# Reordered casts of K and a larger product fill ahead of two groups of transposes in a streaming encoder step

## The chip, the cores and the metric

The kernel runs on one core of a Trainium2 chip. The metric is the device time of one execution in microseconds (us). A time is the median over several executions; one further execution is recorded by the hardware profiler, and all rows below come from that one.

## What is computed

One step of a one-layer encoder over 1024 frames of a new stream and 64 frames of a running one (together T = 1088 columns), in float32. With `x` the normalised input:

```python
q, k, v, gb, gc, h = project_in(xp, w_in[l])            # six pieces of 512 columns each
attn = prompt_attention(q, k, v, rel_bias, lam)         # 4 heads
def probs(qi, ki):
    s = einsum('bqhd,bkhd->bhqk', qi, ki) * scale + bias
    return softmax(where(visible, s, -inf))
p = probs(q[..., :64], k[..., :64]) - lam * probs(q[..., 64:], k[..., 64:])
attn = einsum('bhqk,bkhd->bqhd', p, v)                  # then a norm per head
conv = gb * causal_conv(gc * h, conv_w)
x = LN(alpha * x + concat(attn, conv) @ w_out)
x = LN(alpha * x + relu(x @ w_ff1)**2 @ w_ff2)
```

Each head has two score maps, from two halves of 64 query and key channels. The 64 sample frames also see 256 cached keys and values. K and V are outputs as well.

## The kernel before

**Numbers in two parts.** A float32 matmul operand is held as a high part (a cast to fp32r) and a low part (value minus high part), and a product is made of three matmuls: high by high, high by low, low by high. ACT makes the high parts with a cast, DVE (for weights POOL) the low parts with a subtraction that reads the high part.

**Stages.** First the input norm and the projections of V and of head 0; then the attention, head by head; then the output projection, the first MLP matmul in Strassen form, and the second. The change touches the attention, and in it the K casts that begin during the first stage.

**Projections as fill.** A projection unit (`uq`, `uk`, `uv` with the number of the head, and `uc`, `uh`, `ub` for the convolution) covers three column chunks of 384, 384 and 320. `chunk_gen` (L270) makes one chunk: 24 matmuls, one `yield` after each, into one PSUM bank of tag `pj`, which has two banks. After the last one it calls the evacuation: for K that is `ek` (L331), which copies the chunk to `kf` in SBUF on ACT and calls `dup_split`. 24 products later (`K_LAG`) `store` (L341) transposes the chunk out of `kf` through the one PSUM bank of tag `tr`, for the output.

**`dup_split` (L322)** writes, for both halves m of 64 channels, the high part twice (own partitions and the other half's partitions) into `kh`, and the low part twice into `kl`, so that a score is two matmuls of a query that holds high and low parts stacked. All eight instructions read the PSUM bank of the chunk. For the cached keys `cache` (L372) does the same into `kc` from an SBUF tile `pcs`.

**Attention of a head (`attention_gen`, L703).** The 1024 queries go in four pairs j of 128-row blocks. For each block `score` (L611) makes two score tiles (tag `sc`, two buffers), and `softmax_diff` (L558) turns them into the difference of two softmax maps, tile `a<head><block>e`: DVE adds the bias and takes the row minimum (`a..m`), ACT takes the exponential, DVE scales and combines; L578 is the combination, in halves of 512 columns. `pv_gen` (L631) then goes through groups g of 256 keys: `tr(g)` transposes the group out of the `a..e` tiles of the pair's two blocks (L642) into the PSUM bank of tag `tr`, ACT and DVE split it into `th` (high and low), and `mm(g)` multiplies it with V. The transposes of group g + 1 stand before the products of group g.

**The order of PE is written by hand.** `attention_gen` and `pv_gen` yield a key ahead of each piece of PE work: `("t", j, g)` ahead of the transposes of group g of pair j, `("o", j, g)` ahead of its products, `("s", i, m)` ahead of a score. The main loop asks the table `FILL` for the key and first takes that many products from the fill:

```python
for w in attention_gen(h, qk, v):
    if w is None: ...                       # after the last scores: uk of the next head joins the fill
    for _ in range(fill_of(h, w)):
        next(fill, None)
run(fill)                                   # what is left
```

The fill of a head holds convolution units, then `uv` and `uq` of the next head, and from the last score on `uk` of the next head (72 products), which may not come earlier, since `kh` and `kl` have one buffer. The orders of ACT, DVE, POOL and SP are not written by hand: a scheduler sets them from the program.

Of the kernel before, what the change touches and what calls it, by code (L numbers as in the profile page):

```python
# [13 lines left out]
ALU = mybir.AluOpType  # L14
# [90 lines left out]
def f32(ap):  # L105
    return ap.bitcast(F32)


def build(tc, a, o):
    nc = tc.nc  # L110
    ctx = ExitStack()
    with ctx:
# [191 lines left out]
        with tc.tile_pool(name="pa", bufs=1, side="right", reuse_waits="tile") as pa:  # L304

            def qk_gens(h):
# [11 lines left out]
                kh = pa.tile([128, 2, T], F32R, name=f"kh{h}", tag="kh")  # L318
                kl = pa.tile([128, 2, T], F32R, name=f"kl{h}", tag="kl")
                kf = pa.tile([128, T], F32, name=f"kf{h}", tag="kf")  # L320

                def dup_split(p, h4, l4):  # L322
                    for m in range(2):
                        me = slice(64 * m, 64 * m + 64)
                        ot = slice(64 - 64 * m, 128 - 64 * m)
                        nc.scalar.copy(out=h4[m][me], in_=p[me])
                        nc.scalar.copy(out=h4[m][ot], in_=p[me])
                        nc.vector.tensor_tensor(out=l4[m][me], in0=p[me], in1=f32(h4[m][me]), op=ALU.subtract)
                        nc.vector.tensor_tensor(out=l4[m][ot], in0=p[me], in1=f32(h4[m][me]), op=ALU.subtract)

                def ek(c, t0, n, p):  # L331
                    s = slice(t0, t0 + n)
                    nc.scalar.copy(out=kf[:, s], in_=p[:, :n])
                    dup_split(p[:, :n], [kh[:, m, s] for m in range(2)], [kl[:, m, s] for m in range(2)])
                    later.append([K_LAG, lambda: store("k", c, t0, n)])

                def ev(c, t0, n, p):
# [3 lines left out]
                def store(kind, c, t0, n):  # L341
                    pk = ps.tile([128, 4, 128], F32, name=f"{kind}t{h}{c}", tag="tr")
                    full, rest = divmod(n, 128)
                    if kind == "k":
                        ks = pa.tile([128, 3, 128], F32, name=f"ks{h}{c}", tag="ks", bufs=2)
                        dst, tail = ks[:, :full, :], ks[:64, full, :] if rest else None
                    else:
                        dst, tail = vst[:, t0 // 128:t0 // 128 + full, :], vs[:64, 2, :]
                    for q in range(full + (rest > 0)):
                        w = min(128, n - q * 128)  # L350
                        nc.tensor.transpose(pk[:w, q, :], kf[:, t0 + q * 128:t0 + q * 128 + w], ident)
                    nc.scalar.copy(out=dst, in_=pk[:, :full, :])
                    nc.sync.dma_start(out=o[f"new_{kind}_prompt"][0, 0, t0:t0 + 128 * full, h, :]
                                      .rearrange("(b p) v -> p b v", p=128), in_=dst)
                    if rest:
                        nc.scalar.copy(out=tail, in_=pk[:64, full, :])
                        nc.sync.dma_start(out=o[f"new_{kind}_sample"][0, 0, :, h, :], in_=tail)
# [10 lines left out]
                kc = pa.tile([128, 2, 2, PAST], F32R, name=f"kc{h}", tag="kc")  # L368
# [3 lines left out]
                def cache():  # L372
                    pc = ps.tile([128, 2, 128], F32, name=f"pc{h}", tag="tr")
                    for q in range(2):
                        nc.tensor.transpose(pc[:, q, :], ck[:, q, :], ident)
                    pcs = pa.tile([128, PAST], F32, name=f"pcs{h}", tag="ks", bufs=2)
                    nc.scalar.copy(out=pcs, in_=pc.rearrange("p b t -> p (b t)"))
                    dup_split(pcs, [kc[:, m, 0, :] for m in range(2)], [kc[:, m, 1, :] for m in range(2)])

                held = {}  # L380

# [6 lines left out]
                def lazy(which, c, evac):  # L388
                    yield from chunk_gen(weights(which), x0, c, f"{which}{h}", evac)

                gens = {which: [lazy(which, c, evac) for c in cs]
                        for which, evac, cs in (("uq", eq, range(3)), ("uk", ek, range(3)), ("uv", ev, range(VX // 3, 3)))}
                return (qs, kh, kl, kc, vst, vs), gens, cache, weights, load_v

            with tc.tile_pool(name="p0", bufs=1, reuse_waits="tile") as p0:
# [1100 lines left out]
```

## Time and profile before

| what | value |
|---|---|
| median of 3 timed runs | 1269.4 us (1269.03 to 1272.67) |
| the profiled execution, its own time | 1265.8 us |
| its span, first to last instruction | 1264.0 us |
| mean granted clock of TensorE over the span | 0.984 of full speed |
| DVE busy | 934.0 us (74%) |
| ACT busy | 535.0 us (42%) |
| the chain that ended last, by engine | PE 68%, DVE 11%, ACT 3%, DMA 2% |

How to read it: a busy share is an average over stages with different limits, so the sections of the trace around one place tell more than the table. The chain is the work that ended last, followed back from the last instruction. The granted clock tells which of TensorE's two levels (1.2 or 2.4 GHz) a stretch ran at: 0.50 is the lower and 1.00 the upper. Matmuls overlap in the pipeline, so the distance from one start to the next, not the listed duration, is what a product takes of PE's time.

### The profile page before, as it was taken

What the parts mean: (1) busy time and instruction counts of PE and PEld (TensorE: products, weight loads), DVE (VectorE), ACT (ScalarE), POOL (GpSimd) and SP (SyncE); (2) the same over time, 40 slices, a digit from 0 to 9 for tenths busy, and PEclk for the clock granted to TensorE, in tenths of its full rate; (3) what the DMA queues carried; (4) which work ended last, traced back from release to release, by engine and by line L of the source; (5) the groups of instructions that cost most, each with busy time, mean ns of one, the idle gap of its engine ahead of it and who ended that gap; (6) DMA issues with size and microseconds to landing.
All of it is one profiled execution on the core that took longest, in us unless ns stands there. A gap on an engine that the chain in (4) does not pass through costs nothing.

```text
span 1264.0 us, 18518 instructions
## 1 busy us (share of the span) xinstructions
PE 1201.9 (95%) x7162; PEld 1088.7 (86%) x7162; DVE 934.0 (74%) x1639; ACT 535.0 (42%) x1037; POOL 93.5 (7%) x53
## 2 busy tenths in 40 slices
PE   7999999989999999988999999999999999999994
PEld 5888899989889878868999999999878888888873
DVE  7855955966866977798867676766667688777897
ACT  4454564664664632144333333332444423323523
POOL 3130211111110000000000000000000000000004
PEclk9999999989999999988999999999999999999997
DMA  7861221212222353305453535352895546334203
GB/s 240 277 188 46 85 69 44 70 55 74 65 60 85 98 166 123 107 34 166 143 183 105 184 105 184 105 168 72 280 336 207 199 134 213 126 120 150 67 17 124
DMA packets 118802, 166.61 MB, mean 132 GB/s; under 512 B 9453, under 2 KB 86297, under 8 KB 115130
## 3 DMA queue, kind: packets, MB, share of 16 engines
q1 hardware_dynamic: 118714, 165.43, 39.8%
q8 instruction: 56, 0.92, 0.3%
q14 instruction: 32, 0.26, 0.1%
HBM read 112.20 MB, written 55.57 MB: 133 GB/s over the span
## 4 chain that ended last, share of the span: by engine, by line
PE 68%; DVE 11%; ACT 3%; DMA 2%; issue 1%; SPq 0%; DVEq 0%; ACTq 0%
PE P L1321 21%; PE py L835 7%; PE fa L1005 5%; PE fa L1007 5%; PE fa L1009 5%; PE fc L1009 2%; PE fc L1005 2%; PE fc L1007 2%; PE fb L1007 1%; PE fb L1005 1%; PE fb L1009 1%; DVE hl L1174 1%; DVE wl L1174 1%; PE smP L1360 1%; PE smP L1359 1%
## 5 line engine op out<-in xcount | busy, mean ns | idle before, releaser
L1321 PE MATMUL P<-wh,hh 128*128 128x512 f32 x448 | 174.6, 390 | 3.8 <-DVE t L1247 3.0
L1321 PE MATMUL P<-wl,hh 128*128 128x512 f32 x448 | 174.5, 389 | 0.7 <-DVE wl L1174 0.7
L1321 PE MATMUL P<-wh,hl 128*128 128x512 f32 x448 | 174.4, 389 | 0.0
L1321 PEld LDWEIGHTS P<-wh,hh 128*128 128x128 f32 x448 | 84.1, 188 | 21.9 <-issue 3.2
L1321 PEld LDWEIGHTS P<-wl,hh 128*128 128x128 f32 x448 | 84.1, 188 | 18.6 <-DVE wl L1174 1.1
L1321 PEld LDWEIGHTS P<-wh,hl 128*128 128x128 f32 x448 | 84.1, 188 | 17.5
L1328 DVE TENSOR_TENSOR x<-x,P 128x512 f32<-128x512 f32 x96 | 64.3, 681 | 37.1 <-PE P L1321 36.8
L1172 ACT CAST hh<-hr 128x1024 fp32r<-128x1024 f32 (+1 forms) x28 | 37.2, 1356 | 109.6 <-PE P L1321 105.4
L1005 PE MATMUL fc<-x,wP 128*128 128x272 f32 x256 | 75.0, 293 | 3.1 <-ACT wP L204 2.6
L1009 PE MATMUL fc<-x,wP 128*128 128x272 f32 x256 | 74.9, 293 | 1.6 <-DVE wP L205 1.5
L1007 PE MATMUL fc<-x,wP 128*128 128x272 f32 x256 | 74.7, 292 | 0.0
L1411 POOL TENSOR_TENSOR x<-x 128x1024 f32<-128x1024 f32 x6 | 14.3, 2379 | 792.0 <-DVE x L1409 786.8
L1174 DVE TENSOR_TENSOR hl<-hr,hh 128x1024 fp32r<-128x1024 f32 (+1 forms) x28 | 44.7, 1602 | 27.6 <-ACT hh L1172 27.6
L1005 PEld LDWEIGHTS fc<-x,wP 128*128 128x128 f32 x256 | 49.2, 192 | 4.0 <-ACT wP L204 3.3
L1009 PEld LDWEIGHTS fc<-x,wP 128*128 128x128 f32 x256 | 49.3, 192 | 2.2 <-DVE wP L205 2.2
L1007 PEld LDWEIGHTS fc<-x,wP 128*128 128x128 f32 x256 | 49.2, 192 | 0.0
L1172 ACT CAST hh<-x 128x1024 fp32r<-128x1024 f32 (+1 forms) x13 | 17.6, 1383 | 50.3 <-PE P L1321 40.1
L1005 PE MATMUL fa<-xt3h,wP 128*128 128x272 f32 x128 | 37.1, 290 | 0.9 <-ACT t L1048 0.9
L1005 PE MATMUL fa<-xt4h,wP 128*128 128x272 f32 x128 | 36.9, 288 | 1.1 <-DVE t L1056 1.1
L1007 PE MATMUL fa<-xt2l,wP 128*128 128x272 f32 x128 | 37.4, 293 | 0.0
L1005 PE MATMUL fa<-xt2h,wP 128*128 128x272 f32 x128 | 37.4, 292 | 0.0
L1009 PE MATMUL fa<-xt2h,wP 128*128 128x272 f32 x128 | 37.3, 292 | 0.0
(1483 smaller groups left out, 3780.2 us busy)
## 6 DMA issues: line engine op xcount, KB each, us to landing
hr<-hv SPq DMA_DIRECT2D x19, 1024.0 KB, 5.0
hv<-hS SPq DMA_DIRECT2D x63, 256.0 KB, 4.2
w2B<-in_w_ff SPq DMA_DIRECT2D x11, 1024.0 KB, 6.5
hv<-hb SPq DMA_DIRECT2D x42, 256.0 KB, 2.7
x<-hv SPq DMA_DIRECT2D x9, 1024.0 KB, 5.0
f1r<-in_w_ff SPq DMA_DIRECT2D x17, 512.0 KB, 4.1
f1k<-in_w_ff SPq DMA_DIRECT2D x14, 512.0 KB, 5.1
x<-in_w_ff SPq DMA_DIRECT2D x6, 1024.0 KB, 6.0
```

The lines of the kernel that those rows point to most:

```text
L835: nc.tensor.matmul(py[:, s], lhsT=(ml if m == 2 else mh)[:, e, :], rhs=wo[e][m == 1][:, s], start=(n == 0), stop=(n == len(ops) - 1))
L1005: nc.tensor.matmul(out, lhsT=w[:, 0, k, :], rhs=xh[:, k, cs], start=first and k == 0, stop=False, skip_group_check=not first)
L1007: nc.tensor.matmul(out, lhsT=w[:, 0, k, :], rhs=xl[:, k, cs], start=False, stop=False, skip_group_check=not first)
L1009: nc.tensor.matmul(out, lhsT=w[:, 1, k, :], rhs=xh[:, k, cs], start=False, stop=last and k == 3, skip_group_check=not first)
L1172: nc.scalar.copy(out=hi[q], in_=src[:, w * q:w * q + w])
L1174: nc.vector.tensor_tensor(out=lo[q], in0=src[:, w * q:w * q + w], in1=f32(hi[q]), op=ALU.subtract)
L1321: nc.tensor.matmul(out, lhsT=x[f][:, c], rhs=w[f], start=new and f == 0 and n == 0, stop=f == GP - 1 and n == 2, skip_group_check=not new)
L1328: nc.vector.tensor_tensor(out=dst, in0=dst, in1=out, op=ALU.add)
L1359: nc.tensor.matmul(out, lhsT=st, rhs=wh[f], start=f == 0, stop=False)
L1360: nc.tensor.matmul(out, lhsT=st, rhs=wl[f], start=False, stop=f == GP - 1)
L1411: nc.gpsimd.tensor_tensor(out=y[:rows], in0=y[:rows], in1=b, op=ALU.add)
```

## The change

Three places. The table entries of `("t", 3, 0)`, the transposes of the first group of the last block pair, go from 8 to 22 products in head 0 and from 2 to 20 in head 1. `dup_split` gets a second source `src`, which is `kf` for a K chunk and the same `pcs` for the cached keys. It now first casts each half to its own partitions, then makes all four low parts, and last casts each half to the other half's partitions, reading `src`. The number of instructions is the same.

```diff
-    (0, 'r', 2, 0): 0, (0, 't', 3, 0): 8, (0, 'o', 3, 0): 0, (0, 't', 3, 1): 12, (0, 'o', 3, 1): 0,
+    (0, 'r', 2, 0): 0, (0, 't', 3, 0): 22, (0, 'o', 3, 0): 0, (0, 't', 3, 1): 12, (0, 'o', 3, 1): 0,
...
-    (1, 't', 3, 0): 2, (1, 'o', 3, 0): 0, (1, 't', 3, 1): 11, (1, 'o', 3, 1): 0, (1, 't', 3, 2): 5,
+    (1, 't', 3, 0): 20, (1, 'o', 3, 0): 0, (1, 't', 3, 1): 11, (1, 'o', 3, 1): 0, (1, 't', 3, 2): 5,
...
-                def dup_split(p, h4, l4):
+                def dup_split(p, src, h4, l4):
+
+                    own = [slice(64 * m, 64 * m + 64) for m in range(2)]
                     for m in range(2):
-                        me = slice(64 * m, 64 * m + 64)
-                        ot = slice(64 - 64 * m, 128 - 64 * m)
-                        nc.scalar.copy(out=h4[m][me], in_=p[me])
-                        nc.scalar.copy(out=h4[m][ot], in_=p[me])
-                        nc.vector.tensor_tensor(out=l4[m][me], in0=p[me], in1=f32(h4[m][me]), op=ALU.subtract)
-                        nc.vector.tensor_tensor(out=l4[m][ot], in0=p[me], in1=f32(h4[m][me]), op=ALU.subtract)
+                        nc.scalar.copy(out=h4[m][own[m]], in_=p[own[m]])
+                    for m in range(2):
+                        for part in own[m], own[1 - m]:
+                            nc.vector.tensor_tensor(out=l4[m][part], in0=p[own[m]], in1=f32(h4[m][own[m]]), op=ALU.subtract)
+                    for m in range(2):
+                        nc.scalar.copy(out=h4[m][own[1 - m]], in_=src[own[m]])
...
-                    dup_split(p[:, :n], [kh[:, m, s] for m in range(2)], [kl[:, m, s] for m in range(2)])
+                    dup_split(p[:, :n], kf[:, s], [kh[:, m, s] for m in range(2)], [kl[:, m, s] for m in range(2)])
...
-                    dup_split(pcs, [kc[:, m, 0, :] for m in range(2)], [kc[:, m, 1, :] for m in range(2)])
+                    dup_split(pcs, pcs, [kc[:, m, 0, :] for m in range(2)], [kc[:, m, 1, :] for m in range(2)])
```

The changed file has two lines more in `dup_split`, so every later line has a number that is higher by two (L642 becomes L644).

PE, head 0, ahead of the transposes `t` of block pair 3 (`a06e` and `a07e` are the softmax maps of blocks 6 and 7, `uq1p` the products of head 1's query projection, `vt` the store of V). Before:

```order
L279 MATMUL uq1p_1686<-x_121,uq1h 128x384
L282 MATMUL uq1p_1686<-x_121,uq1l 128x384
L642 MATMUL t_1732<-ident,a06e_1571 128x128
L642 MATMUL t_1732<-ident,a07e_1705 128x128
L642 MATMUL t_1732<-ident,a06e_1571 128x128
L642 MATMUL t_1732<-ident,a07e_1705 128x128
L276 MATMUL uq1p_1686<-x_121,uq1h 128x384
L279 MATMUL uq1p_1686<-x_121,uq1h 128x384
```

and in the changed kernel:

```order
L279 MATMUL uq1p_1686<-x_121,uq1h 128x384
L353 MATMUL vt_1743<-ident,kf_979 128x128 x2
L353 MATMUL vt_1743<-ident,kf_979 64x128
L282 MATMUL uq1p_1686<-x_121,uq1l 128x384
L276 MATMUL uq1p_1756<-x_121,uq1h 128x384
L279 MATMUL uq1p_1756<-x_121,uq1h 128x384
L644 MATMUL t_1759<-ident,a06e_1571 128x128
L644 MATMUL t_1759<-ident,a07e_1705 128x128
L644 MATMUL t_1759<-ident,a06e_1571 128x128
```

The store of V, the end of the first `uq1p` chunk and the first products of the next now stand ahead of the transposes, where before they stood behind them.

DVE, head 1, the low parts `th` of the transposed groups of pair 3 (`kl` is the low part of K for head 2). Before:

```order
L578 SCALAR_TENSOR_TENSOR a17e_2825<-a17e_2833,a17r_2838,a17e_2825 128x512
L205 TENSOR_TENSOR th_2858<-t_2853,th_2858 128x512
L205 TENSOR_TENSOR th_2877<-t_2872,th_2877 128x512
L597 TENSOR_SCALAR r12v<-r12pm 128x256
L205 TENSOR_TENSOR th_2911<-t_2906,th_2911 128x512
```

and in the changed kernel:

```order
L580 SCALAR_TENSOR_TENSOR a17e_2825<-a17e_2833,a17r_2838,a17e_2825 128x512
L205 TENSOR_TENSOR th_2876<-t_2871,th_2876 128x512
L329 TENSOR_TENSOR kl_2041<-uk2p_2850,kh_2040 64x384 x4
L205 TENSOR_TENSOR th_2905<-t_2900,th_2905 128x512
L599 TENSOR_SCALAR r12v<-r12pm 128x256
L205 TENSOR_TENSOR th_2939<-t_2934,th_2939 128x512
```

The four low parts of K's first chunk moved up between the first and the second group's low part; before they stood behind the third.

DVE, start of head 2, from the low part of V (`vl`) to the softmax of block 0 (`a20e` and `a20m` are its map and row minimum, for both halves m). Before:

```order
L205 TENSOR_TENSOR vl_3060<-vst_2043,vh_3059 128x1024
L205 TENSOR_TENSOR r13sl<-r13sq,r13sh 128x256
L563 ISA a20e_3100,a20m_3101<-s_3089,bias_3080 128x128
L563 ISA a20m_3101 128x1
L328 TENSOR_TENSOR kl_2041<-uk2p_2991,kh_2040 64x320
L329 TENSOR_TENSOR kl_2041<-uk2p_2991,kh_2040 64x320
L570 RECIPROCAL a20r_3105<-a20s_3103 128x1
L563 ISA a20e_3108,a20m_3109<-s_3097,bias_3080 128x128
```

and in the changed kernel:

```order
L329 TENSOR_TENSOR kl_2041<-uk2p_2991,kh_2040 64x320 x4
L565 ISA a20e_3100,a20m_3101<-s_3089,bias_3080 128x128
L565 ISA a20m_3101 128x1
L205 TENSOR_TENSOR vl_3060<-vst_2043,vh_3059 128x1024
L205 TENSOR_TENSOR r13sl<-r13sq,r13sh 128x256
L572 RECIPROCAL a20r_3105<-a20s_3103 128x1
L565 ISA a20e_3108,a20m_3109<-s_3097,bias_3080 128x128
```

All four low parts of K's last chunk now precede the first softmax piece, and the low part of V follows it, where before it preceded it.

## Rows read from the trace of the kernel before

**Rows 1.** The page, part 1: busy us (share of the span) and instructions of each engine.
```profile
PE 1201.9 (95%) x7162; PEld 1088.7 (86%) x7162; DVE 934.0 (74%) x1639; ACT 535.0 (42%) x1037; POOL 93.5 (7%) x53
```

**Rows 2.** Waits of PE: line and what it waited for: us, times, longest.
```profile
PE t L642 <- DVE a17e L578: 2.9, 1, 2.9
...
PE t L642 <- DVE a07e L578: 2.0, 1, 2.0
...
PE uk3p L276 <- DVE kl L329: 1.7, 1, 1.7
...
PE ss L625 <- DVE a00r L575: 1.4, 1, 1.4
...
PE ub1p L276 <- DVE kl L329: 1.0, 2, 0.8
...
PE uq0p L276 <- DVE kl L329: 0.9, 1, 0.9
PE uc1p L276 <- DVE kl L329: 0.8, 1, 0.8
```

**Rows 3.** Timeline of PE, head 0: start, us, line, operation [idle before <- releaser].
```profile
154.15 0.27 PE L642 MATMUL t<-ident,a06e 128*128 128x128 f32 x1
156.47 0.48 PE L642 MATMUL t<-ident,a07e 128*128 128x128 f32 x1 [2.05 <-DVE a07e L578]
...
161.43 0.33 PE L642 MATMUL t<-ident,a06e 128*128 128x128 f32 x1 [0.44 <-ACT vs L356]
...
163.03 0.34 PE L279 MATMUL uq1p<-x,uq1h 128*128 128x384 f32 x1
163.21 0.34 PE L282 MATMUL uq1p<-x,uq1l 128*128 128x384 f32 x1
```

**Rows 4.** Windows: length, busy of PE, PEld, DVE, ACT, POOL; PEclk, DMA, GB/s.
```profile
156.47:160.00 3.53, 3.53 (x13) 3.53 (x14) 1.64 (x3) 0.58 (x1) 0.14 (x1) 0.52 0.56 158
256.40:262.30 5.90, 5.90 (x23) 5.80 (x23) 2.74 (x5) 1.17 (x2) 0.00 (x0) 0.51 0.31 89
338.25:344.00 5.75, 3.93 (x28) 3.94 (x28) 5.52 (x12) 3.88 (x10) 0.14 (x1) 1.00 0.54 144
```

**Rows 5.** Timeline of PE, head 1, around the same transposes.
```profile
256.40 0.47 PE L642 MATMUL t<-ident,a17e 128*128 128x128 f32 x1 [2.87 <-DVE a17e L578]
...
260.62 0.41 PE L642 MATMUL t<-ident,a16e 128*128 128x128 f32 x1
...
262.55 0.28 PE L594 MATMUL r12pm<-r12sh,ones 128*128 128x256 f32 x1
```

**Rows 6.** Timelines of DVE (heads 0 and 1) and POOL (the last row).
```profile
155.66 1.42 DVE L578 SCALAR_TENSOR_TENSOR a07e<-a07e,a07r,a07e 128x512 f32<-128x512 f32 x2
...
253.80 2.55 DVE L578 SCALAR_TENSOR_TENSOR a17e<-a17e,a17r,a17e 128x512 f32<-128x512 f32 x1
...
257.73 0.75 DVE L578 SCALAR_TENSOR_TENSOR a17e<-a17e,a17r,a17e 128x512 f32<-128x512 f32 x1
258.50 0.69 DVE L205 TENSOR_TENSOR th<-t,th 128x512 fp32r<-128x512 f32 x1
...
253.46 2.34 POOL L205 TENSOR_TENSOR uc2l<-uc2r,uc2h 128x1024 fp32r<-128x1024 f32 x1 [16.05 <-ACT uc2h L204]
```

**Rows 7.** Timelines of ACT (two rows) and DVE: head 1's K chunk 0.
```profile
178.03 0.48 ACT L333 COPY kf<-uk1p 128x384 f32<-128x384 f32 x1
...
180.54 0.47 ACT L326 CAST kh<-uk1p 64x384 fp32r<-64x384 f32 x1 [1.18 <-DVE kl L329]
...
179.40 0.55 DVE L328 TENSOR_TENSOR kl<-uk1p,kh 64x384 fp32r<-64x384 f32 x1 [1.54 <-ACT kh L327]
...
182.11 0.56 DVE L329 TENSOR_TENSOR kl<-uk1p,kh 64x384 fp32r<-64x384 f32 x1
```

**Rows 8.** Timelines of PE and ACT at the start of head 2.
```profile
280.41 0.39 PE L617 MATMUL s<-kh,qs 128*128 128x256 f32 x1 [0.50 <-DVE a20m L563]
...
280.91 1.03 ACT L204 CAST uh2h<-uh2r 128x1024 fp32r<-128x1024 f32 x1
```

## The prediction

> **What bounds the kernel now.** I read the page's busy line first: PE is busy 1201.9 of 1264.0 us, DVE 74% and ACT 42% [rows 1]. So a change that adds no matmul can only win back time in which PE stands still or runs slowly. The list of what PE waited for comes next; it names such places, and its lines are 1 to 3 us each, so this change is worth at most some 1% to 1.5%. The two longest waits inside the attention are exactly where the table is edited: the first transpose of block pair 3 in head 1 (2.9 us, for a17e) and in head 0 (2.0 us, for a07e) [rows 2]. Then come waits for kl, the low part of K: the projection products of uk3p, ub1p, uq0p and uc1p wait until DVE has read a K chunk out of its PSUM bank, since the tag pj has two banks [rows 2].
>
> What a wait costs beyond itself is in the timelines. In head 0, PE issues the first transpose at 154.15, stands 2.05 us until 156.47 [rows 3], and is slow afterwards. The windows view says why: from 156.47 to 160.00 the granted clock averages 0.52, which is the 1.2 GHz level, before it is back at 2.4 GHz [rows 4]. Head 1 does the same: 2.87 us of waiting, then 5.90 us at 0.51 [rows 4, 5]. A standstill of 1.82 us in head 2, which opens the third window and which the table does not touch, left the clock at 1.00 [rows 4].
>
> **The sum, part by part.** It is made against the profiled execution, 1265.8 us with a span of 1264.0; the median of the timed runs is 3.6 us above it, and I carry the difference over.
>
> *Table, head 0 (fill 8 to 22).* PE gets 14 more products ahead of the transposes. A product is issued every 0.18 us at full clock (163.03 to 163.21 [rows 3]), so they are 2.5 us of work, and PE would reach the transpose at 156.6 plus the store of V, which now stands ahead of it too. DVE finishes the half of a07e that it needs at 155.66 + 0.75 = 156.4 (half of a 1.42 us pair, [rows 6]). The wait of 2.05 goes, and with it the half clock: 3.53 us at 0.52 is a loss of 3.53 x 0.48 = 1.69. The wait of 0.44 for the eviction of the V store, now ahead of the second group [rows 3], moves to the first and I keep it in full, because the same one bank (tag tr) is shared. Gain 2.05 + 1.69 = **3.7 us**. The products come out of the same fill, so nothing is added: the fill of head 0 has 72 K products left behind it, and the pieces at the end of the head are merely shorter.
>
> *Table, head 1 (2 to 20).* 18 products are 3.2 us. Today the first transpose is issued at 256.40 - 2.87 - 0.27 = 253.26 (0.27 is one transpose, [rows 3]); now PE arrives at 253.26 + 3.2 = 256.5, and a17e's first half is done at 253.80 + 2.55 = 256.35 [rows 5, 6]. The wait of 2.87 goes and the half clock with it: 5.90 x 0.49 = 2.89. But here something new is queued. K's chunk 0 now ends four products behind the transposes, so its copy, casts and four low parts stand on ACT and DVE ahead of the second group's cast and low part, as the order rows show. Three short waits come of that. First, eleven products follow the group, so PE is ready for the second group at 256.5 + 0.4 + 11 x 0.18 = 258.9 (0.4 for four transposes is my estimate: today's second group and the six products with V behind it take 1.93 us, most of it at half clock [rows 5], so some 1.1 at full clock). The first group's low part, though, cannot end before 258.50 + 0.69 = 259.2 [rows 6]: a wait of 0.35. Second, DVE then does four K low parts at 0.56 us [rows 7] and 0.69 for the second group's: 259.2 + 2.25 + 0.69 = 262.15. PE is ready for the third group at 259.25 + 1.1 + 0.25 for the norm's two matmuls + 5 x 0.18 = 261.5: a wait of 0.65. Third, the store of K behind the fourth group needs the same bank; the nearest row is the 0.44 of V's eviction in head 0 [rows 3], and I take 0.4. Gain 2.87 + 2.89 - 1.4 = **4.4 us**. All 72 K products are now used up before the last product group, where 8 stood behind it before; that only exchanges places.
>
> *Casts of K.* Today ACT and DVE take turns on one PSUM bank: copy and two casts (178.03 to 179.40), two low parts, then ACT, which stood idle 1.18 us, two more casts, and two low parts until 182.67 [rows 7]. That is 4.64 us. Now the two casts that the low parts need come first, so the four low parts run in one piece: 1.37 + 4 x 0.56 = 3.6 us, and the bank is free 1.0 us earlier. The two remaining casts read kf in SBUF, beside DVE. What a cast costs from there no row shows for 384 columns; the bounds are 0.47 (the same cast from PSUM) and perhaps 0.1 more, and it lies beside 2.25 us of low parts either way, so I cost it at nothing; if that cover were gone, two would cost 1.0 us on ACT. Twelve chunks are shortened; it counts only where PE waits for kl [rows 2]: uq0p 0.9, uc1p 0.8, uk3p 1.0 of its 1.7. Together **2.7 us**.
>
> *Head starts.* Here I take nothing. The last chunk's four low parts now stand on DVE ahead of the second softmax piece of block 0 (in head 2 ahead of the first), so what ub1p's two waits give back, 1.0 us [rows 2], goes into a longer wait for a20m, today 0.50 [rows 8]. For the wait of ss in head 0 (1.4 us, [rows 2]) the chain behind the chunk has the same instructions in another order and ends at the same time.
>
> *Queues.* POOL has the same order, SP only an exchange of two loads; no DMA is added.
>
> Sum 3.7 + 4.4 + 2.7 = 10.8 us: 1255.0 for the profiled execution, **1258.6 us** against the median of 1269.4.
>
> **Rivals.** *The wait moves on.* The low parts of P (cast, then subtract, one bank) set the pace behind the transposes, and both table gains come back as waits at groups two to four. Against it: at head 1's second group, at 260.62, no wait is marked today [rows 5], though PE was slow then, which gave DVE time. It leaves only the 2.7 us: 1266.7.
>
> *POOL in the way.* DVE's half of a17e took 2.55 us where the second took 0.75; it ended when POOL's 2.34 us subtraction, begun at 253.46, had passed [rows 6]. In heads 1 and 2 ACT's casts of the next weights move ahead of casts of V or K, and so do the POOL passes that follow them, beside DVE's low part of V. If that is caught at both starts for 1.8 us each (2.55 - 0.75): 10.8 - 3.6 = 7.2, 1262.2. The Trainium skill (SBUF — State Buffer, Who interferes with whom) says that a VectorE instruction with two SBUF inputs contends with a GpSimd one that reads SBUF and that the loser fully blocks; by that rule this is where it could happen, while K's low parts, which read PSUM and SBUF, are safe.
>
> *One head start goes slow.* In head 2 a weight cast (uh2h, 1.03 us, [rows 8]), kf, K's casts and the four low parts (3.6 us less some 0.3, as the last chunk has 320 columns) now precede a20m: 4.4 us behind the last K product, up to 5.2 if kc's casts are still queued on ACT. PE's way there is six products with V, 13 fill products and two scores, about 3.4 us. So it waits 1.0 to 1.8 us where 0.50 stands; the 1.5 of my sum is in the middle. That is close to the 1.82 that kept the clock and not far from the 2.05 that lost it. At 2.0 us, with the clock lost (2.89), 0.5 + 2.9 = 3.4 us are given back: 1262.0.
>
> *Slower.* The same mechanism at all four heads: the softmax of block 0 behind four low parts, each start waiting over 2 us and then running at half clock, 4 x (2.05 + 2.89) = 19.8 against 10.8: 9 us lost, 1278. It decides if the waits at the starts pass about 2 us. Against it: in heads 0, 1 and 3 the first softmax piece still stands ahead of the low parts.
>
> *More.* All waits for kl, for ss and the small ones vanish: another 5 us, 1253.5.
>
> That the change does not do what it says is excluded by the order rows.
>
> **How the numbers follow.** Forecast 0.60, POOL 0.08, one start slow 0.10, the wait moves on 0.12, slower 0.05, more 0.05. A measurement of this kernel tells about 0.3%, 3.8 us, from no change. Faster by more than that are forecast, POOL, one start and more: 0.83; same is the wait that moves on, 0.12; slower 0.05. The range runs from 1252.5, where every wait goes, to 1265.5, past one or two slow starts; it leaves out the moved wait and the slower case, 0.17.
>
> **What would show it.** Right: no PE wait above 0.6 us for a07e or a17e, granted clock 1.00 in the attention, waits for kl gone but for some 0.7 us at uk3p, the four K low parts in one piece, and a short wait for the second head's P (th). Wrong: a granted clock of 0.5 behind a head's first scores, or the old time in waits for th.

## The result and the profile after

The changed kernel takes 1262.9 us (median of 5 runs, 1259.65 to 1264.19) where the kernel before, timed beside it, takes 1271.7. The ratio is 0.9938, with a 95% interval of 0.992 to 0.9957: 7.9 us faster (5.5 to 10.2), where 10.8 were forecast (a ratio of 0.9915). Here and below the ratio is an estimate from the single runs and not the quotient of the two medians, which lie 8.8 us apart. The profiled execution took 1259.65 us, its span 1257.8, so 6.2 less than the profile before. Busy times hardly moved [rows 1]; the page's first part of the changed kernel:

```profile
PE 1200.6 (95%) x7162; PEld 1087.4 (86%) x7162; DVE 934.3 (74%) x1639; ACT 535.5 (43%) x1037; POOL 94.1 (7%) x53
```

What PE waited for (line, releaser: us in total, times, longest):

```profile
PE t L644 <- DVE th L205: 5.1, 8, 2.6
...
PE s L619 <- DVE a20m L565: 2.1, 1, 2.1
...
PE s L619 <- DVE a00m L565: 1.3, 1, 1.3
...
PE uk3p L276 <- DVE kl L329: 0.7, 1, 0.7
PE pc L377 <- issue: 0.5, 1, 0.5
...
PE ss L627 <- DVE a00r L577: 0.3, 1, 0.3
```

The waits for a07e and a17e, and those for kl at uq0p, uc1p and ub1p, are gone [rows 2]. Two have grown: the one for a20m to 2.05 us, and one within the first row, for the low part of P in head 3, to 2.61. At the start of head 0 the 1.43 us for a00r have become 1.27 for a00m and 0.30 for a00r, and 0.52 us at the transposes of head 1's cached keys (`pc`) are new.

The timeline of PE at pair 3 of heads 0 and 1 (start, us, line, operation) shows the table's work: both transposes follow each other without a stop, and the groups behind wait 0.27 and 0.42 us at most [rows 3, 5].

```profile
157.02 0.33 PE L644 MATMUL t<-ident,a06e 128*128 128x128 f32 x1
157.18 0.27 PE L644 MATMUL t<-ident,a07e 128*128 128x128 f32 x1
...
252.32 0.27 PE L644 MATMUL t<-ident,a16e 128*128 128x128 f32 x1
252.43 0.29 PE L644 MATMUL t<-ident,a17e 128*128 128x128 f32 x1
...
255.26 0.33 PE L644 MATMUL t<-ident,a16e 128*128 128x128 f32 x1 [0.27 <-DVE th L205]
...
258.15 0.33 PE L644 MATMUL t<-ident,a16e 128*128 128x128 f32 x1 [0.42 <-DVE th L205]
```

The windows view (length, busy of PE, PEld, DVE, ACT, POOL, then the granted clock) of these two places, of the start of head 2 and of the place in head 3:

```profile
157.02:160.00 2.98, 2.96 (x18) 2.64 (x19) 2.26 (x5) 1.60 (x4) 0.07 (x1) 1.00 0.78 218
252.32:262.00 9.68, 8.99 (x62) 8.10 (x61) 8.32 (x18) 5.68 (x13) 0.00 (x0) 1.00 0.19 54
272.80:276.20 3.40, 3.40 (x11) 3.40 (x12) 2.57 (x10) 1.38 (x6) 0.00 (x0) 0.51 0.73 213
440.33:443.50 3.17, 3.17 (x14) 3.07 (x15) 1.00 (x2) 0.59 (x1) 0.00 (x0) 0.50 0.02 5
```

Heads 0 and 1 now run at full clock; half clock stands in two new places, each behind one of the two waits.

**Where the time went.** The table gives the time at which PE starts the same instruction in the two profiles, at places where the same number of PE instructions stands ahead of it in both; where the lead grows, time was won.

| PE starts | before | after | lead |
|---|---|---|---|
| first product of uv0p | 78.46 | 79.31 | -0.85 |
| first of uc0p | 90.83 | 90.67 | 0.16 |
| first of uq1p | 151.34 | 151.19 | 0.15 |
| third L276 of uk1p (behind pair 3 of head 0) | 174.71 | 171.33 | 3.38 |
| first of uc1p (behind head 1's K products) | 187.68 | 183.02 | 4.66 |
| first transpose of head 1 | 197.03 | 192.97 | 4.06 |
| first of uk2p | 252.86 | 248.78 | 4.08 |
| first of uh2p (behind the start of head 2) | 303.55 | 296.29 | 7.26 |
| first of uk3p | 353.69 | 346.42 | 7.27 |
| first of ub2p | 369.09 | 360.81 | 8.28 |
| first transpose of pair 3, head 3 | 443.30 | 435.01 | 8.29 |
| norm of pair 3, head 3 | 463.71 | 457.51 | 6.20 |
| last matmul | 1244.65 | 1238.49 | 6.16 |

The first product of uk1p, at 173.67 and 169.57, would show 4.10: but six products with V stand ahead of it before and behind it now, some 0.7 us of work that was only moved.

So the attention won 9.1 us (from -0.85 to 8.29), and head 3 gave back 2.1. The 0.85 at the start differ from profile to profile: by K's first transpose the ten profiles that follow are 0.6 to 2.1 us behind the one of before, with the old casts (1.5 to 1.9 in e1, e2 and e8) as with the new.

**The start of head 2.** The timelines of PE, then DVE, then ACT there:

```profile
270.40 0.34 PE L276 MATMUL ub1p<-x,ub1h 128*128 128x384 f32 x1
272.80 0.56 PE L619 MATMUL s<-kh,qs 128*128 128x256 f32 x1 [2.05 <-DVE a20m L565]
...
267.14 1.72 DVE L329 TENSOR_TENSOR kc<-pcs,kc 64x256 fp32r<-64x256 f32 x4
270.41 2.00 DVE L329 TENSOR_TENSOR kl<-uk2p,kh 64x320 fp32r<-64x320 f32 x4 [1.55 <-ACT kh L326]
272.44 0.29 DVE L565 CUSTOM_DVE_ANT_0 a20e<-s,bias 128x128 f32<-128x128 f32 x1
...
267.89 1.05 ACT L204 CAST uh2h<-uh2r 128x1024 fp32r<-128x1024 f32 x1
...
269.53 0.85 ACT L326 CAST kh<-uk2p 64x320 fp32r<-64x320 f32 x2
```

The score that the first a20e reads was started at 268.74, but a20e stands behind the four low parts, and these behind K's casts, and these behind the cast of uh2h. DVE itself was idle for 1.55 us in between.

**The place in head 3.** ACT's cast of P stands behind a cast of `mr`, which waits for a transfer; PE waits for both:

```profile
438.12 0.94 ACT L204 CAST mh<-mr 128x896 fp32r<-128x896 f32 x1 [3.54 <-DMA mr<-mixd]
438.97 0.58 ACT L204 CAST th<-t 128x512 fp32r<-128x512 f32 x1
...
440.33 0.48 PE L644 MATMUL t<-ident,a36e 128*128 128x128 f32 x1 [2.61 <-DVE th L205]
```

Before, the same wait was 1.98 us and full clock followed it. Nothing that the change touches stands here.

### The profile page after: what moved, and what is told of

Read it like the earlier page. It is cut to its first block, busy times and chain, and to the rows that moved or that the text cites. A ratio compares the mean times of both kernels' runs of the same rounds, so it can differ in the third digit from the quotient of the medians.

```text
span 1257.8 us, 18516 instructions
## 1 busy us (share of the span) xinstructions
PE 1200.6 (95%) x7162; PEld 1087.4 (86%) x7162; DVE 934.3 (74%) x1639; ACT 535.5 (43%) x1037; POOL 94.1 (7%) x53
## 4 chain that ended last, share of the span: by engine, by line
PE 77%; DVE 12%; DMA 4%; ACT 3%; issue 3%; SPq 1%; DVEq 0%; POOL 0%; ACTq 0%; POOLq 0%
PE P L1323 21%; PE py L837 7%; PE fa L1007 5%; PE fa L1009 5%; PE fa L1011 5%; PE fc L1011 3%; PE fc L1007 3%; PE fc L1009 3%; PE fb L1009 1%; PE fb L1007 1%; PE fb L1011 1%; PE v L480 1%; DVE kl L329 1%; PE t L644 1%; PE smP L1361 1%
## 5 line engine op out<-in xcount | busy, mean ns | idle before, releaser
L619 PE MATMUL s<-kh,qs 128*128 128x512 f32 (+3 forms) x96 | 34.1, 358 | 4.3 <-DVE a20m L565 2.1
L1007 PE MATMUL fa<-xt2h,wP 128*128 128x272 f32 x128 | 37.4, 292 | 0.0
```

The costliest lines, as they stand in the source:

```text
L619: nc.tensor.matmul(p[:, c0:c1], lhsT=st, rhs=kh[:, m, c0:c1], start=True, stop=False)
L1007: nc.tensor.matmul(out, lhsT=w[:, 0, k, :], rhs=xh[:, k, cs], start=first and k == 0, stop=False, skip_group_check=not first)
```

## The experiments

Runs e1 to e4, e5 to e8, and e9 with e10 were each timed together, beside runs of the kernel before. In short:

| run | what | median us | ratio to before, interval |
|---|---|---|---|
| e1 | table, head 0 only | 1267.0 | 0.9986, 0.9973 to 0.9999 |
| e2 | table, head 1 only | 1266.1 | 0.9980, 0.9967 to 0.9994 |
| e3 | casts only | 1266.2 | 0.9983, 0.9972 to 0.9994 |
| e8 | both tables, old casts | 1264.1 | 0.9960, 0.9943 to 0.9977 |
| e5 | the change again | 1262.7 | 0.9940, 0.9918 to 0.9962 |
| e6 | the change, late casts from PSUM | 1269.0 | 0.9997, 0.9980 to 1.0014 |
| e9 | old order of casts, late casts from kf | 1260.6 | 0.9939, 0.9915 to 0.9962 |
| e4 | the change, head 2's first score earlier | 1258.8 | 0.9919, 0.9901 to 0.9937 |
| e7 | e4 and more fill in head 3 | 1257.3 | 0.9907, 0.9884 to 0.9930 |
| e10 | e7 and more fill in heads 0 and 2 | 1255.1 | 0.9895, 0.9870 to 0.9920 |

**e1, the table entry of head 0 alone.**

```diff
-(0, 't', 3, 0): 8
+(0, 't', 3, 0): 22
```

> Only the entry of head 0 goes from 8 to 22; casts and head 1 as before. Theory (the terms add up and have their own places): PE's wait for a07e (2.05 us) and the 3.53 us at a granted clock of 0.52 behind it go, 3.7 to 4.0 us, and nothing else moves: the wait of 2.87 us for a17e in head 1 stays, and the waits for kl stay. Faster by 3.7 to 4.0 us, ratio about 0.997. Rival (the fill only moves the wait on): waits for th or the V store of 1 us or more turn up at groups 1 to 3 of pair 3 in head 0, and the gain is under 2 us.

The ratio makes it 1.8 us (0.1 to 3.4), less than expected. In its profile the wait for a07e and the half clock are gone, and the lead grows by 3.3 us between the first product of uq1p and the third L276 of uk1p, not by 3.7 to 4.0: 0.52 us at `pc` are new. No wait for th or the V store turns up in head 0, so the rival falls. By head 1's first transposes 2.8 us of it are left. At head 1's K products the old wait of 0.84 us at uc1p goes, but PE's timeline has a new one a chunk earlier,

```profile
181.79 0.42 PE L276 MATMUL uk1p<-x,uk1h 128*128 128x320 f32 x1 [0.70 <-DVE kl L329]
```

and head 1's scores lose 0.7 us in short stops, two of them listed (0.25 and 0.20 for a11m). With the products of uq1p used up earlier, the low part of head 1's V comes under a POOL pass. The timelines of DVE and POOL in e1, then of DVE before:

```profile
175.92 2.19 DVE L205 TENSOR_TENSOR vl<-vst,vh 128x1024 fp32r<-128x1024 f32 x1 [1.43 <-ACT vh L204]
...
178.46 0.55 DVE L328 TENSOR_TENSOR kl<-uk1p,kh 64x384 fp32r<-64x384 f32 x1
...
174.62 2.40 POOL L205 TENSOR_TENSOR uh1l<-uh1r,uh1h 128x1024 fp32r<-128x1024 f32 x1 [15.98 <-ACT uh1h L204]
...
173.24 1.22 DVE L205 TENSOR_TENSOR vl<-vst,vh 128x1024 fp32r<-128x1024 f32 x1 [1.66 <-ACT vh L204]
```

The low parts of K's first chunk, behind it on DVE, begin 0.49 us after the end of their casts (177.97), and this chunk holds its bank for 5.1 us where it was 4.64. Neither theory had this. In the changed kernel the low part of V takes 2.18 us too, but its casts free the bank at 178.71, ahead of PE's next product at 178.94.

**e2, the table entry of head 1 alone.**

```diff
-(1, 't', 3, 0): 2
+(1, 't', 3, 0): 20
```

> Only the entry of head 1 goes from 2 to 20; casts and head 0 as before. Theory (the slow start of head 2 in the changed kernel, a wait of 2.05 us for a20m and then half clock, comes of the weight cast uh2h and of all four low parts of K's last chunk standing ahead of a20m, so of the table and the new casts together): here uh2h stays behind and only two low parts stand ahead; a20m is waited for 0.5 to 1.5 us and the granted clock stays at 1.00. The table alone gives 2.87 + 2.89 less some 0.7 at the groups behind and 0.5 at the start: faster by 4 to 5 us, ratio about 0.9965. Rival (the table alone, by using K up earlier, makes the slow start): a20m waited for 1.9 us or more with half clock behind it, and the gain is under 3 us.

2.5 us by the ratio (0.8 to 4.2), where 4 to 5 were expected. In the profile the lead grows by 3.8 us from the first product of uk2p to the first of uh2p. No wait for a20m is listed, the clock stays at 1.00, and 1.52 us are waited for a21m instead. The rival falls: the table alone does not make the slow start. In head 0, which this run leaves alone, PE's timeline shows the wait of before [rows 3],

```profile
159.21 0.33 PE L642 MATMUL t<-ident,a07e 128*128 128x128 f32 x1 [2.06 <-DVE a07e L578]
```

but the window behind it shows no half clock [rows 4]:

```profile
159.21:163.00 3.79, 3.35 (x21) 3.06 (x22) 1.63 (x3) 1.51 (x5) 0.14 (x1) 1.00 0.55 147
```

**e3, the casts alone:** the new `dup_split`, both entries as before (8 and 2).

> Only the new order and source of K's casts; both table entries as before. Theory: the wait of 0.9 us at uq0p goes and 1.0 of the 1.7 us at uk3p; at heads 1 and 2 what uc1p (0.84) and ub1p (1.04) no longer wait for comes back for the most part as waits for the first softmax pieces; a20m stays ahead of the low parts of the last chunk, so no half clock there. The two long waits (2.05 and 2.87 us) and their half clock stay. Faster by 2 to 3 us, ratio about 0.998, at the edge of what can be told from no change. Rival (four low parts in one piece hold up the softmax at every head): waits of 1 us and more for a10m, a20m or a30m, half clock at one of them, and no gain or a loss.

2.2 us (0.8 to 3.6). Its profile wins 1.0 at uq0p and 1.0 at uk3p, and 0.4 and 0.5 around the starts of heads 1 and 2; a20m is waited for 0.58 us and a21m 1.34, so ub1p's gain is exchanged for the most part. No half clock at any head's start: the theory stands.

**e8, both entries, old casts.**

> Both table entries, casts as before. Theory: in the attention 2.9 us for head 0 (4.0 less 1.1 given back at K's chunks of head 1, as in e1) and 4 us for head 1 (as in e2), without the slow start of head 2; the waits at uq0p (0.9) and uk3p (1.7) stay. Against the changed kernel it lacks some 3 us of the casts' gain and does not pay the 2 to 3.7 us at the start of head 2: within 1.5 us of the changed kernel, ratio to before about 0.995. Rival (the parts don't add up, since the casts make room for the table): 3 us or more slower than the changed kernel, ratio 0.997 or above.

5.1 us (2.9 to 7.2), and 1.5 us above the changed kernel timed beside it, at the edge of what the theory allows; the intervals overlap. The parts add up within their intervals: 0.9960 by 0.9983 is 0.9943, the change 0.9938 and 0.9940.

**e5, the change again.**

> The changed kernel as it is, on the same chip as the three kernels below, and with a second profile of it. Theory: what belongs to the order comes again to 0.1 us: no wait for a07e or a17e, a wait of 2.05 us for a20m in head 2, 0.69 us for kl at uk3p. What is of the execution differs: the waits for DMAs in the first 85 us, the wait for th in head 3 (1.98 to 2.8 us in six profiles), and whether half clock follows a wait of some 2 us. Ratio to before 0.992 to 0.996. Rival: the order alone decides about the clock; then half clock follows the 2.05 us again, and nothing follows where nothing followed.

The order's waits came back to 0.02 us: 2.04 for a20m, 0.67 at uk3p. Half clock followed the 2.04 again, so here the rival is not refuted; in head 3 half clock followed 2.39 us, in e8 and e6 it did not follow 2.58 and 2.48. The attention's gain in this profile is 9.2 us (from -0.97 to 8.24). Its span is 2.9 us longer than that of the first profile all the same, and all of that is lost behind head 3: so kernels are compared by the lead through the attention, not by the span of one profile.

**e6, the two late casts from PSUM:** `src` is the bank again, everything else as changed.

```diff
-dup_split(p[:, :n], kf[:, s], ...)
+dup_split(p[:, :n], p[:, :n], ...)
```

> The changed kernel, but the two late casts of a K chunk read the PSUM bank again instead of kf in SBUF. Theory (the order of the casts gives the gain, the source only sets where the scheduler puts things): a chunk's four low parts still run in one piece, 3.6 us from the copy to their end, and the wait at uq0p stays away. In head 2 a20m now stands behind the low part of V and one more subtraction too, 1.65 us, so it is waited for 3 us or more and half clock follows: 1 to 3 us slower than the changed kernel. Rival (the source matters by itself, two engines at one bank): the copy to the end of the low parts takes 4.2 us or more, and 0.6 us or more comes back at uq0p and uk3p each.

The whole gain is gone: 6.4 us above the changed kernel, where I had expected 1 to 3. The low parts do run in one piece, 3.6 us from the copy at 183.38 to their end at 187.01, and a20m is waited for, with half clock behind. But the rival is right in the main: the bank is not free then, and at uq0p and uk3p 1.7 us each come back where the rival asked for 0.6. The list of PE's waits now has ACT's late cast as the releaser at the chunks:

```profile
PE s L619 <- DVE a20m L565: 2.5, 1, 2.5
...
PE uk3p L276 <- ACT kh L331: 1.7, 1, 1.7
PE uq0p L276 <- ACT kh L331: 1.7, 1, 1.7
PE uc1p L276 <- ACT kh L331: 1.7, 1, 1.7
PE ub1p L276 <- ACT kh L331: 1.5, 1, 1.5
```

and ACT's timeline shows how a late cast runs:

```profile
182.03 0.96 ACT L331 CAST kh<-uk1p 64x384 fp32r<-64x384 f32 x2 [2.78 <-DVE kl L329]
...
186.76 1.04 ACT L204 CAST ub1h<-ub1r 128x1024 fp32r<-128x1024 f32 x1 [2.04 <-issue]
187.83 0.96 ACT L331 CAST kh<-uk1p 64x384 fp32r<-64x384 f32 x2
```

It does not run beside the low parts: it waits for the end of all four, and, standing late, it can come behind a weight cast too. The built programs say the same, in what the instruction waits for (e6, then the changed kernel):

```
L331 CAST kh1_977<-uk1p0_1899 64x384 [waits DVE_49]
L331 CAST kh1_977<-kf1_979 64x384 [waits Activation_49]
```

So it is a wait that the scheduler has put into the program. The Trainium skill (PSUM — Partial Sum Buffer, PSUM bank collisions raise a hardware error) states that ScalarE and VectorE may not access the same bank in the same 32 partitions at once, two reads included, and that the compiler's scheduler adds a dependency between two such instructions. The wait of 2.78 us agrees, but goes further: the late cast of one half's partitions also stood until the low parts of the other half were done.

e8, timed beside it, differs from e6 in the order of the casts alone, and is 4.9 us faster, the two intervals apart: with the late casts on the bank the new order cost time.

**e9, the old order, late casts from kf.**

```diff
                     for m in range(2):
                         nc.scalar.copy(out=h4[m][own[m]], in_=p[own[m]])
-                    for m in range(2):
+                        nc.scalar.copy(out=h4[m][own[1 - m]], in_=src[own[m]])
                         for part in own[m], own[1 - m]:
                             nc.vector.tensor_tensor(out=l4[m][part], in0=p[own[m]], in1=f32(h4[m][own[m]]), op=ALU.subtract)
-                    for m in range(2):
-                        nc.scalar.copy(out=h4[m][own[1 - m]], in_=src[own[m]])
```

> Both table entries, and per half of K the order of before (cast, cast to the other half's partitions, two low parts), but the second cast reads kf in SBUF. Theory (what frees the PSUM bank sooner is the source: its readers take turns, so the bank is held for the sum of the reads, and kf takes 0.96 us of them away; the order of the casts is worth nothing): from the copy to the last low part 3.6 to 4.1 us, the wait at uq0p gone, some 0.7 us left at uk3p, and, with only two low parts ahead of a20m, no slow start in head 2: at least as fast as the changed kernel, ratio to before 0.991 to 0.994. Rival (the order counts): 4.3 us or more from the copy to the last low part, the waits at uq0p, uc1p and uk3p back to 0.6 us and more, and slower than the changed kernel, 0.996 or above.

By the ratios as fast as the changed kernel (0.9939 against 0.9938 and 0.9940, each to some 3 us), so no gain of the order of the casts, half of what the change is named for, can be seen. The wait at uq0p is gone, 0.72 us are left at uk3p. Head 1's second K chunk in e9, timelines of ACT, then DVE:

```profile
178.86 0.49 ACT L333 COPY kf<-uk1p 128x384 f32<-128x384 f32 x1
179.23 0.48 ACT L326 CAST kh<-uk1p 64x384 fp32r<-64x384 f32 x1
179.73 1.04 ACT L327 CAST kh<-kf 64x384 fp32r<-64x384 f32 x2
180.89 0.47 ACT L326 CAST kh<-uk1p 64x384 fp32r<-64x384 f32 x1
...
179.74 1.11 DVE L329 TENSOR_TENSOR kl<-uk1p,kh 64x384 fp32r<-64x384 f32 x2 [0.98 <-ACT kh L326]
181.40 1.14 DVE L329 TENSOR_TENSOR kl<-uk1p,kh 64x384 fp32r<-64x384 f32 x2 [0.54 <-ACT kh L326]
```

and in the changed kernel:

```profile
179.34 0.49 ACT L335 COPY kf<-uk1p 128x384 f32<-128x384 f32 x1
179.71 0.96 ACT L326 CAST kh<-uk1p 64x384 fp32r<-64x384 f32 x2
180.70 1.04 ACT L331 CAST kh<-kf 64x384 fp32r<-64x384 f32 x2
...
180.70 2.26 DVE L329 TENSOR_TENSOR kl<-uk1p,kh 64x384 fp32r<-64x384 f32 x4 [2.00 <-ACT kh L326]
```

From the copy to the last low part it is 3.68 us in e9 and 3.62 in the changed kernel; before, head 1's first chunk took 4.64 [rows 7]. In both the bank serves the copy, two casts and four low parts, one after the other; the two late casts run beside. So a chunk's time does not depend on the order either. In head 2, e9 waits 0.73 us for a20m, at full clock.

**e4, head 2's first score three products earlier.**

```diff
-(2, 's', 0, 0): 5, (2, 's', 1, 0): 3
+(2, 's', 0, 0): 2, (2, 's', 1, 0): 6
```

> The changed kernel with the first score of head 2 three products earlier: entry (2, s, 0, 0) from 5 to 2 and (2, s, 1, 0) from 3 to 6. By the order of DVE a20m then stands ahead of the four low parts of K's last chunk instead of behind them. Theory (the wait for a20m is one of order: DVE stood idle for 1.5 us before those low parts, long after the score was done): the wait of 2.05 us and the 1.7 us lost at half clock go, some 1 us of it comes back at the next score of head 2, since a20m of the second half still stands behind the low parts and the low part of V; 2 to 3 us faster than the changed kernel, ratio to before about 0.992. Rival (the start is short of work, whoever goes first): the wait moves by under 0.5 us and the clock still falls.

DVE's timeline shows a20e taken in the idle time, at 268.89 instead of 272.44:

```profile
268.89 0.29 DVE L565 CUSTOM_DVE_ANT_0 a20e<-s,bias 128x128 f32<-128x128 f32 x1
...
270.40 2.00 DVE L329 TENSOR_TENSOR kl<-uk2p,kh 64x320 fp32r<-64x320 f32 x4 [1.22 <-ACT kh L326]
...
274.38 0.29 DVE L565 CUSTOM_DVE_ANT_0 a20e<-s,bias 128x128 f32<-128x128 f32 x1
```

The long wait and the half clock are gone; 1.09 us come back at the fourth score and 0.46 at the norm behind. The lead at uh2p is 1.5 us larger than in the changed kernel, less than the 2 to 3 expected; the ratio is 0.0019 lower (2.4 us), and the two intervals overlap.

**e7, more products ahead of head 3's second transposes:** e4, and

```diff
-(3, 't', 3, 1): 9, (3, 'o', 3, 3): 31
+(3, 't', 3, 1): 20, (3, 'o', 3, 3): 20
```

> The kernel of e4 with 11 more products of the output projection ahead of the second group of transposes of pair 3 in head 3: entry (3, t, 3, 1) from 9 to 20, (3, o, 3, 3) from 31 to 20. Theory (the wait for th there is one for a cast that stands behind the cast of mr, which waits for a DMA; it is covered by any product that is ready): 11 products of 0.23 us cover 2.5 us, the wait of 2.53 us and the half clock behind it go; 2.5 to 4 us faster than e4, ratio to before 0.989 to 0.990. Rival (the products run dry: those of the output projection need the same late DMA): the wait stays, under another name.

The longest wait for th falls from 2.53 to 0.59 us, the clock there is 1.00, and a wait of 0.51 for th comes up at the products:

```profile
PE t L644 <- DVE th L205: 2.5, 7, 0.6
...
PE o L661 <- DVE th L205: 0.5, 1, 0.5
```

In its profile, PE's lead at the norm of pair 3 is 3.1 us larger than in e4, within the 2.5 to 4 expected. The ratio moved by 0.0012 only (1.5 us), and the two intervals overlap.

**e10, more products at two head starts:** e7, and

```diff
-(2, 's', 1, 1): 14, (2, 'o', 0, 0): 33, (0, 's', 1, 0): 0, (0, 'o', 0, 0): 30
+(2, 's', 1, 1): 20, (2, 'o', 0, 0): 27, (0, 's', 1, 0): 7, (0, 'o', 0, 0): 23
```

> The kernel of e7 with six more products ahead of the fourth score of head 2 (entry (2, s, 1, 1) from 14 to 20, (2, o, 0, 0) from 33 to 27) and seven more ahead of the third score of head 0 ((0, s, 1, 0) from 0 to 7, (0, o, 0, 0) from 30 to 23). Theory (both waits are for a softmax piece and covered by any product): the six go past the wait of 1.10 us only if they stand ahead of it; that score is the third one of head 2, so they don't, and only the 0.45 us behind it go; in head 0 the wait of 1.27 us for a00m goes. 1.2 to 1.7 us faster than e7, ratio to before about 0.9895. Rival (the softmax chain sets the pace at a head's start): the waits move to the transposes of the first pair, and nothing is gained.

I had miscounted: the entry is the fourth score's, the one that waited 1.10 us. So both waits go: 0.2 us is left for a20m, and none is listed for a00m or a00r. From uv0p to uh2p the lead grows by 1.8 us more than in e7. At 13.3 us (10.1 to 16.5) under the kernel before, it has the lowest ratio of the set, though one that lies within e7's interval.

## Why the prediction was right, and where not

- **Table, head 0:** 3.7 forecast, 3.2 in the profile, wait and half clock both gone. So is the 0.44 for the V store, which the sum kept; against it stand the 0.52 at `pc`, which the sum did not have, and some 0.4 that the list puts to no wait. What the step did not say is that 1.69 of it is there only in executions whose clock falls behind the wait: e2 and e3 had the wait without it.
- **Table, head 1:** 4.4 forecast. The 2.87 and 2.89 went; of the 1.4 set against them only 0.27 and 0.42 came, and the K store did not wait. That is 5.1: the step's waits were sized twice too long.
- **Casts of K:** 2.7 forecast, 2.7 in the profile: 1.0 at uq0p, 1.0 at uk3p, and 0.7 around head 1, where the lead goes from 3.38 to 4.66 at uc1p and then back to 4.06, as head 1's scores lose 0.6 in short stops (0.19 of it listed, for a11m). The duration, 3.6 us, was right. That it comes of the two needed casts standing first was wrong: e9 has it without that order, and e6, with that order, frees the bank only after the late casts. It comes of taking two reads off the bank.
- **Head starts:** zero forecast, and this is the step that failed. I let a20m be waited for 1.0 to 1.8 us, counting 4.4 to 5.2 us from the last K product to a20m. That product started at 266.93 and a20e at 272.44, 5.5 us, since kc's casts, the cast of uh2h and a copy all came ahead of K's last casts on ACT. The wait of 2.05 us, and 3.40 us at a clock of 0.51 behind it, are what the prediction gives as a sign that it is wrong, and the rival **one head start goes slow**, which had been given 0.10 and 1262.0 us. Of waits and lost clock this stretch had 2.87 + 2.89 + 0.50 + 0.28 + 0.76 = 7.3 us before and has 0.69 + 2.05 + 1.67 = 4.4 now. That is 2.9, and the lead grew by 3.2 from uk2p to uh2p, not by the 4.4 of the sum. The start of head 0 came as said: 1.57 us stand there where 1.43 stood.
- **POOL in the way:** it came at one of the two starts that the rival named, and PE did not wait for it. In head 1 the low part of V took 2.18 us, 1.10 of them under POOL's pass, where it took 1.22 before, clear of POOL; in head 2 it took 1.23, clear of POOL again. The first half of a17e took 2.62 us under POOL's pass, as before [rows 6].
- **The wait moves on:** it did not come.
- **Not in the forecast at all:** head 3. The 2.1 us lost there in the profile are the execution's: of ten profiles with this wait, six show half clock behind it, with the old casts (e1) as with the new, and the 1.98 us of the kernel before are the shortest of the ten. The timed runs, which average over that, gave 7.9 us.

So the attention won 9.1 of the 10.8 us: of the 1.7 that lack, 0.5 are head 0's and 1.2 those of head 1 with the start of head 2. The forecast's sign and range held, though its 10.8 lies just outside the measured interval, and its likeliest case did not come about: a rival did, offset in part by waits behind head 1's transposes that were half as long as forecast. That the rival's 1262.0 us stand beside 1261.5, the measured ratio on the median that the forecast started from (0.9938 x 1269.4), is luck in part: the start of head 2 took less than its 3.4 us, and head 0 and head 3, which the rival left alone, took something too.

## What to carry to other kernels

In these kernels a PSUM bank was held for the sum of its reads by ACT and DVE, 4.64 us with all of them and 3.6 with two fewer: copy it out once and let every reader that is not urgent take the copy. When fill is pulled forward to cover one wait, look at who is then first in the queue of the engine that serves the next one; on an engine with a fixed order, a wait with that engine idle in between (1.55 us here) went with three products in another place. Compare two profiles only at points with the same work ahead: a moved piece looks like a gain. And the half clock behind a wait of two microseconds came in some executions and not in others, so it is to be counted with a chance, not as part of the wait.

## What was not expected of the hardware

The same wait at the same place is followed by half clock in one execution and not in the next. For a07e in head 0 it was 2.05 us and a granted clock of 0.52 before [rows 3, 4], but 2.06 (e2) and 2.03 us (e3) with 1.00. In head 3, 2.41 (e2), 2.48 (e6) and 2.58 us (e8) were not followed by it, 2.39 (e5) and 2.53 us (e4) were. Even 1.43 us, the wait for ss in head 0, was followed by it in e2, while the same 1.43 left the clock at 1.00 before and in e1 and e8; in e6, 1.27 us for a00m and then 0.53 for a00r were followed by it. What decides it was not tried.

The low part of V, which reads two operands in SBUF on DVE, loses most of the time that it shares with a POOL pass. Over the twelve profiles it takes 1.22 to 1.23 us with no such time, 1.25 to 1.27 with 0.2 us (head 0), 1.66 to 1.67 with 0.58 (head 3), and 2.18 to 2.19 with 1.10 (head 1, wherever head 0's table entry was changed).
